# Output products in attention's last steps, and up-weight splits ahead of the last quotient

## The chip, the cores and the metric

One core of one Trainium2 chip runs the kernel. The metric is the device time of one execution in microseconds (us); for a set of runs it is their median. TensorE (PE in the profile) multiplies matrices, ScalarE (ACT) and VectorE (DVE) work on tiles element by element and read TensorE's results from PSUM, GpSimd (POOL) works on tiles in SBUF, and SyncE (SP) issues most of the DMAs.

## The reference

A decoder block on 1024 tokens of width 1024, all in float32:

```python
proj = rmsnorm(h) @ w_in                         # q, k, v, u, gate, forget
att  = forgetting_attention(q, k, v, log_f)      # 8 heads of 64, causal softmax
sg   = chunked_spatial_gating(gelu(u), gelu(gate), ...)
h = h + concat([att, sg]) @ w_out
a, g = split(conv3(rmsnorm(h) @ w_up) + conv_b)  # 2 x 2816 columns
h = h + (silu(g) * a) @ w_down
return rmsnorm(h) * norm_final_g
```

## The kernel before

**Number format.** Every float32 operand of a matmul is split into a high part (a cast) and a low part (source minus high part), and a product is three matmuls: high x high, high x low, low x high. `split_w` makes both parts of a weight tile: the high one on ScalarE (L160), the low one on VectorE (L166). The large projections are done by a Strassen-Winograd scheme on 2 x 2 blocks, so they need sums of blocks of the weights and of the activations (S1 to S4, T1 to T4).

**Attention** runs in 40 steps, five for each of eight heads (`STEPS`). A step n transposes the softmax weights of step n + 1 on TensorE (`turn_p`, L1038); ScalarE (L1039) and VectorE (L1040) split the result into a tile `pt` of three buffers. Then it does the value products of step n (`values`, L1054), and in between the logits of the next head, while there is one (`logits_mm`, L984 and L985). The order on TensorE is written by hand: `seq` chains every matmul to the one before. The last head has no logits beside it, so steps 35 to 39 hold transposes and values alone.

**The quotient.** A head's row sums are transposed (`row_tail`, L941), copied (L942), written to DRAM by a DMA that ScalarE issues (L943), and read back spread over 64 partitions by a DMA on SyncE (L944). `pair_half` divides for two heads: multiply by the reciprocals (L953 or L957), cast (L954 or L958), low part (L955 or L959). Three pairs go through GpSimd; the last, `pair_half(3, ...)`, through VectorE and ScalarE, tokens 512 to 1023 first, then 0 to 511. Its result is `attT[3]`.

**Output projection** (`wmm`, L1303 to L1305). For token tile tt (128 tokens) and half hf (512 columns), four head pairs k of three matmuls each add up in one PSUM bank. The order of the token tiles is 0, 4, 1, 5, 2, 3, 6, 7. For the first four tiles the pairs k = 0, 1, 2, eight groups of nine matmuls, come first; they do not need `attT[3]`. Then, tile by tile: the rest of the products, the addition of the residual (`hadd`, L1313, one operand in PSUM), the norm (`norm2`, L1320 to L1323), and one tile later the transposes of the normed tile (`flip`, L1341) with their evacuations. These matmuls are not chained by `seq`; a planner orders them by its costs.

**First up weights.** `upw_a(i)` loads two blocks of weight column i and `split` splits them (i = 0 and 1 ahead of time) into tiles `wha`. `upw_b(i, ..., True)` then makes four sums for each i on GpSimd (L1275, L1276, L1277, L1283), in place over the raw blocks. `wha` lies in a pool that takes the place of attention's pool `early`, after its release.

**Order.** Queues are in order. Where the code doesn't say, a planner places instructions by its own costs; `after(tc, later, earlier)` adds an edge of order without a semaphore, `behind(inst, key)` the same from a table `gates`, and `act.on = dve.on = True` chains all that follows on these engines.

Of the kernel before, what the change touches and what calls it, by code (L numbers as in the profile page):

```python
# [8 lines left out]
F32 = mybir.dt.float32  # L9
# [60 lines left out]
def block_kernel(ctx: ExitStack, tc: tile.TileContext, xT, xtok, wuv, wuh, wv0, wva, wvk, wvl, wqk, cpk, bfv,  # L70
# [5 lines left out]
    sml = ctx.enter_context(tc.tile_pool(name="sml", bufs=4))  # L76
    early = tc.alloc_tile_pool(name="early", bufs=1)
# [13 lines left out]
    BUFS = {"x1": 2, "x2": 2, "t3": 1, "t2": 1, "t01": 1, "V": 4, "H": 4, "wy": 2, "gg": 2,  # L91
# [4 lines left out]
    def sb(tag, shape, dt=F32):  # L96
        return (raws if tag == "raw" else late if tag in LATE else early).tile(shape, dt, tag=tag, bufs=BUFS[tag], name=nm(tag))

# [58 lines left out]
    def split_w(src, hl, hi_eng="act", lo_eng="dve"):  # L157
        h, l = hl
        if hi_eng == "act":
            act.copy(h, src)  # L160
# [5 lines left out]
        return eng.tensor_tensor(out=l, in0=src, in1=f32(h), op=ALU.subtract)  # L166

    gates = {}
# [9 lines left out]
    def xset(tags):  # L178
        return [sb(t, [P, 2, 2, 512], F32R) for t in tags]
# [5 lines left out]
    def xs(n, hl, k):  # L185
        return XS[n][k // 2][:, hl, k % 2, :]

    def x2(n, hl, j):
        return XS[n][j][:, hl, :, :]
# [433 lines left out]
    def emit(t, dst, i, parts, src=None):  # L623
        for o in parts:
            if dst is kd:
                dve.tensor_tensor(out=t[:, 1, o], in0=t[:, 1, o], in1=rb[:, o], op=ALU.mult)
            x = t[:, 1, o] if src is None else src
            act.copy(t[:, 0, o].bitcast(F32R), x)
            floors[dst is kd] = dve.tensor_tensor(out=t[:, 1, o], in0=x, in1=t[:, 0, o], op=ALU.subtract)
            for j in range(2):  # L630
                floors["sp"] = sp.dma_start(out=dst[2 * i + j].rearrange("s d t -> d s t")[:, :, o], in_=t[j * 64:(j + 1) * 64, :, o])

# [80 lines left out]
    floors = {}  # L713
# [16 lines left out]
    xy = sb("x1", [P, 2, 1024])  # L730
    xl = sb("pt", [P, 1024])
    sp.dma_start(out=xl, in_=vx[0])
    after(tc, sp.dma_start(out=xy, in_=vx[1:3].rearrange("a p c -> p a c")), floors["ld"])
    for i, o in ((0, ALU.subtract), (1, ALU.add)):
        after(tc, dve.tensor_tensor(out=xy[:, i], in0=xy[:, i], in1=xl, op=o), newest[0])
    vw["S1"] = pairs(l21)

# [130 lines left out]
    def head_loads(h):  # L868
        ab = sb("x1", [P, 2, 1024], F32R)
        abs_[h] = ab  # L870
        hh = h % 2
        sp.dma_start(out=f32(ab[:, 0, :]), in_=qd[h].rearrange("s d t -> (s d) t"))
        for s in range(2):
            sp.dma_start(out=f32(ab[s * 64:s * 64 + 64, 1, :]), in_=kd[h, 0])
# [10 lines left out]
    va_, vb_, vc_ = xy[:, 0], xy[:, 1], xl  # L885
# [61 lines left out]
    def pair_half(p, o):  # L947
# [8 lines left out]
        else:  # L956
            dve.tensor_tensor(out=f[:, 0, o], in0=f[:, 0, o], in1=f[:, 1, o], op=ALU.mult)  # L957
# [5 lines left out]
    psa = tc.alloc_tile_pool(name="psb", bufs=4, space=bass.MemoryType.PSUM, reuse_waits="tile")  # L963

    def place():
        return psa.tile([P, 1024], F32, tag="L", bufs=2, name=nm("pl"))
# [9 lines left out]
    def logits_mm(h, j, ps):  # L976
        A, B, A2, B2 = abs_[h][:, 0, :], abs_[h][:, 1, :], a2s[:, h % 2, :], b2s[:, h % 2, :]
# [135 lines left out]

    STEPS = [[(h, g) for g in GROUPS[n:n + 2]] for h in range(8) for n in range(0, 9, 2)]
# [35 lines left out]
    for n, step in enumerate(STEPS):  # L1150
# [33 lines left out]
        out_copy = None  # L1184
        for c, (g, pt, js) in enumerate(zip(step, now, NEXT[s])):
# [30 lines left out]
    for o in (slice(512, 1024), slice(0, 512)):  # L1216
        pair_half(3, o)


    after(tc, act.activation(pad[:, 0:1], eps, AF.Sqrt), last_copy)  # L1220


    ss2 = cst.tile([P, 8], F32, name="ss2")

    early.release()
    psa.release()
    psa = tc.alloc_tile_pool(name="psc", bufs=4, space=bass.MemoryType.PSUM, reuse_waits="tile")
    upl = tc.alloc_tile_pool(name="upl", bufs=1, reuse_waits="tile")
    xtp = tc.alloc_tile_pool(name="xtp", bufs=1, reuse_waits="tile")

    g2b = xtp.tile([P, 1024], F32, name="g2b")
    sp.dma_start(out=g2b, in_=g2r.to_broadcast((P, 1024)))
    XB = {}

    def xb_tile(pool_, n):
        XB[n] = pool_.tile([P, 2, 4, 512], F32R, tag="x" + n, bufs=1, name="x" + n)

    for n in ("B11", "B21", "T2", "T3"):
        xb_tile(upl, n)

    def ut_(pool_, tag, shape, dt, bufs):
        return pool_.tile(shape, dt, tag=tag, bufs=bufs, name=nm(tag))

    xt = {n: xtp.tile([P, 4, 512], F32, tag="xt" + n, name="xt" + n) for n in ("B11", "B21", "B22")}
# [4 lines left out]
    def upw_a(i):  # L1249
# [15 lines left out]
        return out, split  # L1265

# [32 lines left out]
    def wmm(tt, hf, ps, ks_):  # L1299
        ts_ = slice(tt * P, (tt + 1) * P)  # L1300
        for k in ks_:
            w = wo[k][hf]
            pe.matmul(ps, attT[k][:, 0, ts_], w[:, 0, :], start=(k == 0), stop=False)  # L1303
            pe.matmul(ps, attT[k][:, 0, ts_], w[:, 1, :], start=False, stop=False)
            pe.matmul(ps, attT[k][:, 1, ts_], w[:, 0, :], start=False, stop=(k == 3))  # L1305

# [26 lines left out]
    def flip(tt):  # L1333
# [3 lines left out]
        for kh in range(2):  # L1337
            ps = sbank()
            for j in range(4):
                k = 4 * kh + j  # L1340
                pe.transpose(ps[:, j * P:(j + 1) * P], xn[tt][:, k * P:(k + 1) * P], ident)  # L1341
# [58 lines left out]
    def psq(tag):  # L1400
        return psa.tile([P, 512], F32, tag="b" if tag in "ab" else "s", bufs=4, name=nm("q" + tag))
# [217 lines left out]
    banks = [psa.tile([P, 512], F32, tag="b" if j < 4 else "s", bufs=4, name="k%d" % j) for j in range(8)]  # L1619

    RING = {"xr": (upl, "sg", 4), "xh": (upl, "wha", 4), "wh": (upr, "whb", 6)}
# [168 lines left out]
    raws.release()  # L1790
    psa.release()
# [53 lines left out]
```

## Time and profile before

| what | value |
| --- | --- |
| median of 3 runs | 1046.32 us (1046.3 to 1047.15) |
| profiled execution | 1046.16 us, span 1044.4 us |
| mean granted TensorE clock | 0.998 |
| last value products end, first output product starts | about 357.5 us |
| last quotient's parts | 362.4 to 365.0 us |
| first residual addition of the output projection | 374.75 us |
| first products of the up projection | 407.06 us |

The page gives busy times and the chain that ended last; the timeline gives each instruction's start, duration, lines and tiles (`out<-in`), and in brackets how long its engine had idled and what ended that. Start-to-start distances on TensorE tell more than its busy time, since matmuls overlap in the record.

### The profile page before, as it was taken

Reading aid. Unit: us, or ns where it says so; the run is one execution under the profiler, and the core shown is the slowest. Engines: PE = TensorE matmul, PEld = TensorE weight load, DVE = VectorE, ACT = ScalarE, POOL = GpSimd, SP = SyncE. Lnnn points to the kernel's source line nnn. Section 1 sums busy time; section 2 is a strip of 40 time slices with the busy share of each in tenths; the row PEclk is TensorE's granted clock in tenths of the full one; section 3 lists DMA queues with packets and bytes.
Section 4 is the critical chain, followed back from the end, with each engine's and each line's share of the span. In section 5 each row is a group of like instructions: output and inputs, shape, how many; then the busy total and the mean of one; then the engine's idle time right before and its main releaser. Section 6 shows DMA issues by size and latency. Waiting matters only on the chain.

```text
span 1044.4 us, 14270 instructions
## 1 busy us (share of the span) xinstructions
PE 1036.8 (99%) x4998; PEld 870.0 (83%) x4998; DVE 893.3 (86%) x1302; ACT 562.8 (54%) x1003; POOL 222.6 (21%) x167
## 2 busy tenths in 40 slices
PE   9999999999999999999999999999999999999997
PEld 7988888988888888788888888888888888888886
DVE  6899887988888779998999998898997866997774
ACT  6777632457776747644444444443544544454654
POOL 0000232500322540353334323323331000000000
PEclk9999999999999999999999999999999999999999
DMA  9622558885745533231354431332422998333432
GB/s 331 235 85 95 153 156 250 232 259 170 203 135 167 201 134 130 81 120 62 121 168 146 142 121 67 127 111 73 129 81 83 325 337 292 112 92 101 144 118 101
DMA packets 67452, 161.66 MB, mean 155 GB/s; under 512 B 8095, under 2 KB 9239, under 8 KB 67381
## 3 DMA queue, kind: packets, MB, share of 16 engines
q1 hardware_dynamic: 67108, 160.72, 47.9%
q8 instruction: 39, 0.64, 0.3%
q14 instruction: 33, 0.26, 0.1%
q10 hardware_dynamic: 272, 0.04, 0.0%
HBM read 115.68 MB, written 45.05 MB: 154 GB/s over the span
## 4 chain that ended last, share of the span: by engine, by line
PE 98%; DVE 1%; ACT 0%; issue 0%; ACTq 0%; DVEq 0%
PE k L1656 20%; PE qc L1396 12%; PE qa L1396 11%; PE qd L1396 11%; PE qb L1396 5%; PE pb L270 5%; PE ps L270 5%; PE pb L1054 3%; PE pb L1038 3%; PE qc L509 2%; PE qd L509 2%; PE qa L509 2%; PE pl L984 2%; PE ps L853 2%; PE pl L985 2%; PE pf L1078 1%
## 5 line engine op out<-in xcount | busy, mean ns | idle before, releaser
L1656 PE MATMUL k<-whb,wha 128*128 128x512 f32 (+1 forms) x936 | 209.9, 387 | 0.0
L1656 PEld LDWEIGHTS k<-whb,wha 128*128 128x128 f32 x936 | 174.1, 188 | 35.8 <-DVE wha L166 0.2
L1396 PE MATMUL qc<-xT,whb 128*128 128x512 f32 x540 | 129.8, 389 | 0.1
L1396 PE MATMUL qa<-xB,wha 128*128 128x512 f32 x528 | 127.5, 390 | 0.0
L1396 PEld LDWEIGHTS qc<-xT,whb 128*128 128x128 f32 x540 | 101.3, 188 | 21.5 <-ACT whb L160 0.5
L1396 PEld LDWEIGHTS qa<-xB,wha 128*128 128x128 f32 x528 | 98.8, 188 | 20.9 <-DVE wha L166 0.4
L160 ACT CAST wha<-sg 128x512 fp32r<-128x512 f32 x77 | 47.8, 622 | 96.6 <-PE k L1656 84.9
L160 ACT CAST whb<-sg 128x512 fp32r<-128x512 f32 x82 | 50.5, 618 | 87.9 <-PE qc L1396 67.6
L166 DVE TENSOR_TENSOR wha<-sg,wha 128x512 fp32r<-128x512 f32 x77 | 52.8, 688 | 39.0 <-ACT wha L160 38.9
L1396 PE MATMUL qd<-xB,whb 128*128 128x512 f32 x264 | 63.7, 389 | 0.0
L1396 PE MATMUL qd<-xT,whb 128*128 128x512 f32 x264 | 63.7, 390 | 0.0
L1396 PE MATMUL qb<-xT,whb 128*128 128x512 f32 x252 | 61.0, 390 | 0.0
L166 DVE TENSOR_TENSOR whb<-sg,whb 128x512 fp32r<-128x512 f32 x82 | 57.0, 697 | 4.4 <-ACT whb L160 4.3
L1280 POOL TENSOR_TENSOR sg<-raw 128x512 f32<-128x512 f32 x20 | 31.0, 1550 | 139.4 <-DVE whb L166 76.2
L1039 ACT CAST pt<-pb 128x512 fp32r<-128x512 f32 x72 | 40.1, 583 | 36.0 <-PE pb L1038 23.7
L1396 PEld LDWEIGHTS qd<-xT,whb 128*128 128x128 f32 x264 | 49.5, 188 | 10.5 <-DVE u L1503 0.3
L1396 PEld LDWEIGHTS qd<-xB,whb 128*128 128x128 f32 x264 | 49.6, 188 | 10.3
L1396 PEld LDWEIGHTS qb<-xT,whb 128*128 128x128 f32 x252 | 47.2, 188 | 10.0 <-DVE whb L166 0.3
L1040 DVE TENSOR_TENSOR pt<-pb,pt 128x512 fp32r<-128x512 f32 x72 | 47.3, 686 | 9.6 <-ACT pt L1039 8.9
L1054 PE MATMUL pb<-pt,V 128*128 128x512 f32 (+3 forms) x192 | 49.4, 362 | 0.4 <-DVE pt L1040 0.3
L1283 POOL TENSOR_TENSOR sg<-sg,raw 128x512 f32<-128x512 f32 x20 | 33.3, 1664 | 63.5 <-DVE whb L166 63.5
L1281 POOL TENSOR_TENSOR sg<-sg,raw 128x512 f32<-128x512 f32 x20 | 35.1, 1756 | 47.2 <-issue 44.6
(431 smaller groups left out, 2247.6 us busy)
## 6 DMA issues: line engine op xcount, KB each, us to landing
raw<-wup SPq DMA_DIRECT2D x44, 512.0 KB
sg<-hx SPq DMA_DIRECT2D x77, 256.0 KB
hx<-hs SPq DMA_DIRECT2D x44, 256.0 KB
hx<-ca SPq DMA_DIRECT2D x35, 256.0 KB
xT<-wdn SPq DMA_DIRECT2D x28, 256.0 KB
x<-kd SPq DMA_DIRECT2D x24, 256.0 KB
A<-xtok SPq DMA_DIRECT2D x8, 512.0 KB
raw<-wqk SPq DMA_DIRECT2D x8, 512.0 KB
```

The lines of the kernel that those rows point to most:

```text
L160: act.copy(h, src)
L166: return eng.tensor_tensor(out=l, in0=src, in1=f32(h), op=ALU.subtract)
L270: pe.matmul(banks[m], xs(n, xi, k)[:, ms], w[:, wi, :], start=(first and k == 0 and c == 0 and (own or m % 2 == 0)), stop=(k == 3 and c == ...
L509: pe.matmul(ps, w[:, wi, ks], xs(n, xi, k), start=(first and c == 0), stop=(c == 11), skip_group_check=True)
L1038: seq(pe.transpose(ptr[:, o:o + P], places[g[0], j // 2][j % 2][:, k * P:(k + 1) * P], ident))
L1039: casts.append(act.copy(pt[:, 0, :], ptr))
L1040: los.append(dve.tensor_tensor(out=pt[:, 1, :], in0=ptr, in1=f32(pt[:, 0, :]), op=ALU.subtract))
L1054: seq(pe.matmul(po[half][:, o:o + w], lhs, pt[:, s, c:c + w], start=(new and s == 0), stop=(s == 1 and (half, k) in ((1, 6), (0, 3))), ski ...
L1281: pool.tensor_tensor(out=s[1], in0=s[0], in1=a11, op=ALU.add)
L1283: pool.tensor_tensor(out=s[3], in0=s[1], in1=a12, op=ALU.add)
L1396: pe.matmul(ps, w[:, wi, ks], xb[:, xi, k, :], start=(first and n == 0), stop=(n == 11), skip_group_check=True)
L1656: pe.matmul((banks[bk + m] if ps is None else ps)[:, o], xh[:, xi, ms], wh[:, wi, o], start=((first and p_ == 0 or new) and n == 0), stop= ...
```

## The change

- `wmm` moves ahead of the loop over the steps and is chained by `seq`. Token tile 0, half 0, takes its k = 0, 1, 2 in steps 36, 37 and 39, after the transposes and before the values of the step. Its bank comes from a PSUM pool that replaces the one of the logits after their last use.
- After attention only four more groups of nine are done ahead of k = 3: (4, 0), (0, 1), (4, 1) and (1, 0).
- The first up weights (i = 0, 1) are split right behind the last values: their casts come after the last evacuation of values, and the first multiply of the last quotient comes after the last of the four subtractions. The load of the square root's table comes after the last cast. For this the tiles of `wha` move into the pool of the logits' operands (tag `x1`, four buffers of half the size), which stays allocated.
- The flips have written places between half tiles, chained by `seq`, except the last.
- The partial sums of the values are loaded by two DMAs instead of one, ahead of the last six stores of queries and keys; their two additions come behind the last splits and the last query subtraction.

```diff
     def split_w(src, hl, hi_eng="act", lo_eng="dve"):
         if hi_eng == "act":
-            act.copy(h, src)
+            cast[:] = [act.copy(h, src)]
...
-    xy = sb("x1", [P, 2, 1024])
+    xy = [sb("x1", [P, 1024]) for _ in range(2)]
     xl = sb("pt", [P, 1024])
     sp.dma_start(out=xl, in_=vx[0])
-    after(tc, sp.dma_start(out=xy, in_=vx[1:3].rearrange("a p c -> p a c")), floors["ld"])
-    for i, o in ((0, ALU.subtract), (1, ALU.add)):
-        after(tc, dve.tensor_tensor(out=xy[:, i], in0=xy[:, i], in1=xl, op=o), newest[0])
+    for i in range(2):
+        ld = sp.dma_start(out=xy[i], in_=vx[1 + i])
+        after(tc, ld, floors["ld"])
+        for st in stores[-6:]:
+            after(tc, st, ld)
+    adds = [dve.tensor_tensor(out=xy[i], in0=xy[i], in1=xl, op=o) for i, o in ((0, ALU.subtract), (1, ALU.add))]
     vw["S1"] = pairs(l21)
+    for x in adds:
+        after(tc, x, newest[0])
+        after(tc, x, floors[False])
...
         else:
-            dve.tensor_tensor(out=f[:, 0, o], in0=f[:, 0, o], in1=f[:, 1, o], op=ALU.mult)
+            m = dve.tensor_tensor(out=f[:, 0, o], in0=f[:, 0, o], in1=f[:, 1, o], op=ALU.mult)
+            if gates:
+                after(tc, m, gates.pop("own"))
             act.copy(t[:, 0, o], f[:, 0, o])
...
+    def wmm(tt, hf, ps, ks_):
+        ts_ = slice(tt * P, (tt + 1) * P)
+        for k in ks_:
+            w = wo[k][hf]
+            for n, (a, b) in enumerate(((0, 0), (0, 1), (1, 0))):
+                seq(pe.matmul(ps, attT[k][:, a, ts_], w[:, b, :], start=(k == 0 and n == 0), stop=(k == 3 and n == 2)))
+
+    banks8 = {}
+    EARLY = {36: (0,), 37: (1,), 39: (2,)}
...
+        if n == 35:
+            psl.release()
+            psl = tc.alloc_tile_pool(name="psc", bufs=4, space=bass.MemoryType.PSUM, reuse_waits="tile")
+            banks8[0, 0] = lbank()
+        if n in EARLY:
+            wmm(0, 0, banks8[0, 0], EARLY[n])
         for c, (g, pt, js) in enumerate(zip(step, now, NEXT[s])):
...
             for n in names:
-                t = ut_(upl, "wha", [P, 2, 512], F32R, 4)
+                t = ut_(base, "x1", [P, 2, 512], F32R, 4)
                 split_of[n] = split_w(wr[:, ("A11", "A12").index(n), :], (t[:, 0], t[:, 1]))
-                behind(split_of[n], "sums" if i < AHEAD else "hg")
+                if i < AHEAD:
+                    after(tc, cast[0], last_copy)
+                else:
+                    behind(split_of[n], "hg")
...
+    WA = [upw_a(i) for i in range(AHEAD)]
+    W = [a[1](("A11", "A12")) for a in WA]
+    gates["own"] = split_of["A12"]
+    for o in (slice(512, 1024), slice(0, 512)):
+        pair_half(3, o)
+
+
+    after(tc, act.activation(pad[:, 0:1], eps, AF.Sqrt), cast[0])
...
     def flip(tt):
-            ps = sbank()
+            ps = bank()
             for j in range(4):
                 k = 4 * kh + j
-                pe.transpose(ps[:, j * P:(j + 1) * P], xn[tt][:, k * P:(k + 1) * P], ident)
+                t = pe.transpose(ps[:, j * P:(j + 1) * P], xn[tt][:, k * P:(k + 1) * P], ident)
+                if tt < 7:
+                    seq(t)
...
-    WA = [upw_a(i) for i in range(AHEAD)]
-    W = [WA[0][1](("A11", "A12"))]
-    first = (0, 4, 1, 5)
-    banks8 = {(tt, hf): (bank() if hf == 0 else sbank()) for tt in first for hf in range(2)}
-    for hf in range(2):
-        for tt in first:
-            wmm(tt, hf, banks8[tt, hf], (0, 1, 2))
-    W.append(WA[1][1](("A11", "A12")))
+    early_ = ((0, 0), (4, 0), (0, 1), (4, 1), (1, 0))
+    for tt, hf in early_[1:]:
+        banks8[tt, hf] = bank() if tt == 1 else lbank()
+        wmm(tt, hf, banks8[tt, hf], (0, 1, 2))
     WB = [upw_b(0, W[0], True), upw_b(1, W[1], True)]
-    prev = None
+    FLIP = {(1, 1): 0, (5, 0): 4, (2, 0): 1, (3, 0): 5, (6, 0): 2, (7, 0): 3, (7, 1): 6}
     for tt in (0, 4, 1, 5, 2, 3, 6, 7):
         hload(tt)
         for hf in range(2):
-            if tt in first:
-                wmm(tt, hf, banks8[tt, hf], (3,))
-                hadd(tt, hf, banks8[tt, hf])
-            else:
-                ps = bank()
-                wmm(tt, hf, ps, range(4))
-                hadd(tt, hf, ps)
-        norm2(tt)
-        if prev is not None:
-            flip(prev)
-        prev = tt
+            ps = banks8[tt, hf] if (tt, hf) in early_ else bank() if tt == 1 else lbank()
+            wmm(tt, hf, ps, (3,) if (tt, hf) in early_ else range(4))
+            hadd(tt, hf, ps)
+            if hf:
+                norm2(tt)
+            if (tt, hf) in FLIP:
+                flip(FLIP[tt, hf])
```

`lbank()` takes one of four banks of the pool that replaces the logits' places, `bank()` one of the four others.

More of the change, by code (lines that the diff above doesn't have):

```diff
@@ L96, in sb @@
     def sb(tag, shape, dt=F32):
-        return (raws if tag == "raw" else late if tag in LATE else early).tile(shape, dt, tag=tag, bufs=BUFS[tag], name=nm(tag))
+        return (base if tag == "x1" else raws if tag == "raw" else late if tag in LATE else early).tile(shape, dt, tag=tag, bufs=BUFS[tag], name=nm(tag))
     def bank():
@@ L178, in xset @@
     def xset(tags):
[L179 removed]
+        r = []
+        for t in tags:
+            if t == "x1":
+                r.append([sb(t, [P, 2, 512], F32R) for _ in range(2)])
+            else:
+                b = sb(t, [P, 2, 2, 512], F32R)
+                r.append([b[:, 0], b[:, 1]])
+        return r
     RAW = {n: [sb(t, [P, 2, 512]) for t in tags] for n, tags in (
@@ L1618, in block_kernel @@
     ssa = dn.tile([P, 1], F32, name="ssa")
-    banks = [psa.tile([P, 512], F32, tag="b" if j < 4 else "s", bufs=4, name="k%d" % j) for j in range(8)]
-    RING = {"xr": (upl, "sg", 4), "xh": (upl, "wha", 4), "wh": (upr, "whb", 6)}
+    banks = [lbank() if j < 4 else bank() for j in range(8)]
+    RING = {"xr": (upl, "sg", 4), "xh": (base, "x1", 4), "wh": (upr, "whb", 6)}
     def dt_(tag, shape, dt):
```

67 lines of the change are left out of this document (31 added, 36 removed).

## Prediction

> **What bounds the kernel now.** I read the page from the top (busy shares, then the chain that ended last), then what TensorE waited for over the whole span.
>
> ```profile
> span 1044.4 us, 14270 instructions
> PE 1036.8 (99%) x4998; PEld 870.0 (83%) x4998; DVE 893.3 (86%) x1302; ACT 562.8 (54%) x1003; POOL 222.6 (21%) x167
> PE 98%; DVE 1%; ACT 0%; issue 0%; ACTq 0%; DVEq 0%
> PE ps L126 <- DVE pad L137: 1.3, 1, 1.3
> ```
>
> TensorE is the bound, and no instruction of it is removed. A change can only pay by closing small waits and can only cost by opening new ones. "Busy" hides small waits, because a matmul's modelled end overlaps the next; they show as start-to-start steps that are too long. The yardsticks, from the chain, are twelve 512-column matmuls in 2.72 us (0.227 each) and eight transposes in 0.87 us (0.109 each). Here are attention's last steps, first as TensorE's timeline, then as the chain:
>
> ```profile
> 425.34 2.72 PE qd L1396 x12
> 352.87 0.87 PE pb L1038 x8
> ...
> 351.71 1.16 PE L1054 MATMUL pb<-pt,V 128*128 128x512 f32 x4
> 354.68 0.27 PE L941 MATMUL pb<-ident,rs 128*8 128x128 f32 x1
> 357.45 0.45 PE L1303 MATMUL pb<-whl,A 128*128 128x512 f32 x1
> ...
> 354.25 0.60 ACT pt L1039
> 354.87 0.70 DVE pt L1040
> 355.64 0.60 ACT pt L1039
> 356.25 0.70 DVE pt L1040
> ```
>
> From the values of step 36 (351.71) to the first output product (357.45) pass 5.74 us. The work in them is 8 matmuls of 512 columns, 4 of 384, 4 of 256, 4 of 128 and 13 transposes: at 0.227 us in proportion to columns, and 0.109, that is 1.82 + 0.68 + 0.45 + 0.23 + 1.42 = 4.60 us. So 1.1 us is waiting, on the ScalarE cast and VectorE subtraction of the transposed weights, as the chain says.
>
> **The change part by part.**
>
> *Three groups in steps 36, 37 and 39.* Nine products of 0.227 us, 2.04 us in all, leave the stretch after attention and enter these steps. Filled perfectly they would hide 1.1 us; unfilled, 0. I take 0.95: almost all the waiting is late in the stretch, behind the insertions, but the pt ring has three buffers, so a later cast waits for the values just pushed back. Attention then ends at 357.45 + 2.04 - 0.95 = 358.54. The transposed row sums (354.68) stand behind two of the groups: 1.36 us of inserted work, less about 0.15 of covered waits, make the last quotient's transfers about 1.2 us later.
>
> *The last quotient and the up splits.* Before:
>
> ```profile
> 358.87 0.45 SPq L944 DMA_DIRECT2D H<-rsd  x1
> 357.65 0.58 ACT L1062 COPY H<-pb 64x512 f32<-64x512 f32 x1 [0.82 <-PE pb L1054]
> 358.25 1.28 ACT L1220 ACT_TABLE_LOAD   x1
> 358.26 0.68 DVE L1063 TENSOR_TENSOR H<-pb,H 64x512 f32<-64x512 f32 x1 [0.60 <-ACT H L1062]
> 362.36 1.29 DVE L957 TENSOR_TENSOR H<-H 128x512 f32<-128x512 f32 x2 [3.41 <-DMA H<-rsd]
> 363.08 1.22 ACT L958 CAST G<-H 128x512 fp32r<-128x512 f32 x2 [3.33 <-DVE H L957]
> 363.74 1.29 DVE L959 TENSOR_TENSOR G<-H,G 128x512 fp32r<-128x512 f32 x2
> 374.32 0.39 PE L1305 MATMUL pb<-G,G 128*128 128x512 f32 x1
> ```
>
> The quotient is ready at 363.74 + 1.29 = 365.03, and TensorE first reads its low part at 374.32, after 72 products that need only heads 0 to 5. The change leaves 36 between attention's end and that group. TensorE would be there at 358.54 + 36 x 0.227 + 2 x 0.227 = 367.17. Meanwhile the four splits (four casts, four subtractions) come into VectorE's 3.41 us of idling, and the first quotient multiply is ordered behind the last of them. The gap looks as if it holds them: four subtractions at 0.6 us. But what follows the first of them matters:
>
> ```profile
> 364.95 0.68 DVE L166 TENSOR_TENSOR wha<-raw,wha 128x512 fp32r<-128x512 f32 x1
> 366.15 1.78 DVE L166 TENSOR_TENSOR wha<-raw,wha 128x512 fp32r<-128x512 f32 x1
> 367.85 1.77 DVE L166 TENSOR_TENSOR wha<-raw,wha 128x512 fp32r<-128x512 f32 x1
> ...
> 365.71 1.67 POOL L1275 TENSOR_TENSOR raw<-raw,raw 128x512 f32<-128x512 f32 x1 [12.72 <-DMA pt<-hpd]
> 369.04 1.74 POOL L1277 TENSOR_TENSOR raw<-raw 128x512 f32<-128x512 f32 x1
> 370.74 1.29 POOL L1283 TENSOR_TENSOR raw<-sg,raw 128x512 f32<-128x512 f32 x1
> 374.75 0.69 DVE L1313 TENSOR_TENSOR pt<-pb,pt 128x512 f32<-128x512 f32 x1 [5.12 <-PE pb L1305]
> ```
>
> GpSimd's eight sums of up weights overwrite the raw weights in place, so the first starts 0.08 us after the first subtraction ends (365.63). From there the two engines take turns. A subtraction with both inputs in SBUF takes 1.78 us instead of 0.68, and each GpSimd sum 1.67 to 1.74 instead of 1.29 alone. The two ends 367.93 and 369.62 set the period: 1.69 us. The addition that reads PSUM keeps its 0.69 us. Before, only two subtractions that nobody waited for met the sums. In the new order GpSimd starts ahead of the quotient, so two subtractions, both multiplies and both quotient subtractions (two SBUF inputs each) meet them, and eight sums outlast six such turns.
>
> The page "SBUF — State Buffer" of the Trainium skill (section "Who interferes with whom") states the same as a rule: VectorE with two SBUF inputs and a GpSimd read exclude each other, and the later one blocks for the whole instruction. Taking turns at the lone durations, 0.68 + 1.29 = 1.97 us, it would put the sum 5 x 0.28 = 1.4 us higher than the measured turns do.
>
> The sum by measured rows: last copy 358.54 + 0.20 = 358.74; its addition 0.61 later, 359.35; first subtraction from 359.96 to 360.64; third ends 2.30 after the first (365.63 to 367.93), 362.94; fourth 364.63; the multiplies 366.32 and 368.01; the subtractions 369.70 and 371.39. The row sums land at 362.3 + 1.2 = 363.5, ahead of the first multiply, and the casts (0.61) lie beside VectorE's turns. The table load, now behind the casts, ends near 363. TensorE reads the low part at 371.45 instead of 367.17: it stands 4.3 us, some 2 before the first product of the group (its cast ends 0.61 after the second multiply) and the rest before the third.
>
> Against before: at 374.32 TensorE had 74 of these products behind it, at 371.45 it has 47. The missing 27 x 0.227 = 6.13 us bring it level at 377.58, 3.26 us late. That already contains the 0.95 of the first part.
>
> *Norms and flips, in written order.* Work is the same. VectorE's additions begin at about 371.9 (0.43 behind that product, as before) instead of 374.75, while TensorE is 3.3 us later, so VectorE has some 6 us more lead. What can be had here:
>
> ```profile
> 380.38 0.88 PE ps L1341 x8
> 383.55 0.61 PE ps L1341 x4
> 385.79 1.06 PE ps L1341 x8
> ...
> 428.96 0.60 PE qd L1396 x2
> 429.56 0.83 PE qb L1396 x3
> 441.59 0.51 ACT whb L160
> ...
> 416.00:424.00 8.00, 8.00 (x37) 6.62 (x36) 8.00 (x10) 7.34 (x10) 0.00 (x0) 1.00 0.00 0
> ```
>
> Two flips are long by 0.17 and 0.19 us, against 0.44 for four and 0.87 for eight transposes: 0.35 goes. Around 428 to 442 stand 0.15 + 0.15 (two at 0.60, three at 0.83, against 0.227 each) and at most the 0.51 of the cast at 441.59. VectorE is full from 416 on (8.00 of 8.00 in the window), but this follows the last flip, which keeps its place behind TensorE's products, so I take 0, with 0.8 as the bound. The first flip now follows the products of (1, 1), at 377.1, some 3.9 us after token tile 0's second addition ends. Before, from that end (374.75 + 2 x 0.68 = 376.1) to the flip at 380.38 it took 4.3 with other tiles' additions in between, so a wait of 0 to 0.4 can open; VectorE is less crowded, and I take 0.
>
> *Edits at nothing.* The x1 tiles and the split tiles change pools with as many buffers. The value partial sums:
>
> ```profile
> 176.79 0.90 SPq L733 DMA_DIRECT2D x<-vx  x1
> 182.44 4.37 SPq L631 DMA_DIRECT2D kd<-G  x4
> 185.34 0.68 DVE L629 TENSOR_TENSOR G<-G 128x512 f32<-128x512 f32 x1
> 185.94 2.35 DVE L735 TENSOR_TENSOR x<-x,pt 128x1024 f32<-128x1024 f32 x2
> ```
>
> One load becomes two, about 0.9 us more on SyncE's queue; the six stores now ordered behind them issue from 182.44, 4.7 us later anyway. The two additions already run behind the last query subtraction, which becomes their order. If that cover went, the 2.35 us would delay the values' evacuation.
>
> *Sum.* 3.26 - 0.35 = +2.9 us. The profiled execution took 1046.16 us (1.76 around its span) and gives 1049.06; the median, 0.16 above it, gives 1049.2.
>
> **The rivals.**
>
> *GpSimd is out of the way* (its tiles still held by attention's, or its queue ordered otherwise). Then the fourth subtraction ends at 362.5, the quotient at 363.5 + 0.6 + 0.61 + 0.6 + 0.69 = 366.0, before 367.17. What remains is -0.95 - 0.35 = -1.3 us: 1045.0. For it speaks that the trace cannot show which old tile the sums' first output covers; against it, that before nothing but the first subtraction held them. Held for half the window, +0.8: 1047.1.
>
> *VectorE's lead pays* (the other side, faster). Without the collision all small waits go: 1.1 + 0.35 + 0.8 = 2.25 us, and 1044.1 remains. It decides only if the quotient's low part stands by 367.2 and the 0.8 us at 428 to 442 was backlog. VectorE's 8.00 of 8.00 speaks for it, the last flip's place against.
>
> *The fill fills nothing.* The pt ring moves with the inserted products, and 0.95 is lost. This adds 0.95 to each case: 1050.1 with the collision, 1046.0 without.
>
> *A slow clock after the stall.* The clock row shows 1.00 in every window, and the longest wait of the trace is 1.3 us; 4.3 us in two parts is outside what it shows. At the start there is such a phase:
>
> ```profile
> 1.29 3.59 PE ps L126 x8
> ```
>
> The eight warming matmuls and the five after them step by about 0.43 us, 0.2 more each; paying that once is 13 x 0.2 = 2.6 us: 1051.8. The page "TensorE: Matmul & The Clock Gate" of the Trainium skill (Part 1) puts the drop after an idle window of about 3.4 us; each of the two halves is shorter, and no row here tests it.
>
> **How the numbers follow.** Collision as summed 0.53, GpSimd out of the way 0.25, half-way 0.08, VectorE's lead 0.08, slow clock 0.06. A bound of 0.2% is 2.1 us, about what a measurement of this kernel can tell from no change: faster is below 1044.2, slower above 1048.4. Slower: 0.47 of the collision (its own range, by 0.95 of fill and 0.2 us per turn, is 1048.1 to 1050.2; the lowest part, 0.06, falls inside) and 0.06: 0.53. Same: 0.25 + 0.08 + 0.06 = 0.39. Faster: 0.08. The range runs from 1044.4, under the case without collision, to 1050.6; outside lie the fastest case, the slow clock and some tails, under 0.2.
>
> **What would show it.** Right: subtractions of the first up weights from about 360, the later ones near 1.7 us with GpSimd busy beside them; quotient multiplies (128x512, H) also near 1.7 us; TensorE idle about 2 us twice, released by the quotient's cast and then its subtraction; first hidden-state addition near 371.9. Wrong: multiplies at 0.69 us and the first addition near 367.6, or GpSimd's first sum behind the quotient. The fill is right if the first product of token tile 4 starts near 358.5.

## Result: 0.6% slower, and the profile after

The changed kernel takes 1052.83 us (median of 6 runs, 1052.21 to 1053.37) against 1046.46 us before; the ratio is 1.0060 (95% interval 1.0047 to 1.0073). Its profiled execution took 1052.44 us. The forecast was 1049.2, with a range up to 1050.6: the direction was right, but the loss is 6.4 us where 2.9 were forecast, more than twice as much.

The head of the page and TensorE's waits over the whole span (line that waited, line that released it, total us, times, longest us):

```profile
span 1050.7 us, 14270 instructions
PE 1038.0 (99%) x4998; PEld 870.4 (83%) x4998; DVE 896.6 (85%) x1302; ACT 564.6 (54%) x1003; POOL 223.4 (21%) x167
PE pk L1140 <- ACT G L975: 2.0, 1, 2.0
PE pk L1140 <- DVE G L976: 1.9, 1, 1.9
PE pb L838 <- DVE G L55: 1.0, 3, 0.6
```

The busy share of TensorE is 99% in both kernels and shows nothing. The waits do: two at the output products (L1140) for the last quotient, as forecast, and three at L838, the transposes of the gated values ("gate transposes" below), 143 us ahead of the first step that the prediction gives a price (208.6 against 351.7 us).

Around the quotient, VectorE's and GpSimd's timeline:

```profile
361.92 4.68 DVE L167 TENSOR_TENSOR x<-raw,x 128x512 fp32r<-128x512 f32 x4
366.53 3.46 DVE L972 TENSOR_TENSOR H<-H 128x512 f32<-128x512 f32 x2
369.91 3.42 DVE L976 TENSOR_TENSOR G<-H,G 128x512 fp32r<-128x512 f32 x2
374.10 0.69 DVE L1346 TENSOR_TENSOR pt<-pk,pt 128x512 f32<-128x512 f32 x1 [0.78 <-PE pk L1140]
362.69 1.67 POOL L1316 TENSOR_TENSOR raw<-raw,raw 128x512 f32<-128x512 f32 x1 [8.07 <-DVE x L167]
364.44 1.61 POOL L1318 TENSOR_TENSOR raw<-raw 128x512 f32<-128x512 f32 x1
```

Before, two multiplies took 1.29 us and two quotient subtractions 1.29 us; now 3.46 and 3.42. GpSimd's first sum starts 0.08 us behind the first split subtraction (361.92 + 0.69) and from there the engines take turns, as forecast. TensorE's timeline and granted clock at the same place (a row of windows: length, then busy us of PE, PEld, DVE, ACT, POOL with counts, then the granted clock, DMA share, GB/s):

```profile
360.38 0.91 PE L1140 MATMUL pk<-whl,A 128*128 128x512 f32 x3
...
367.95 0.84 PE L1140 MATMUL pb<-G,G 128*128 128x512 f32 x3
370.78 0.70 PE L1140 MATMUL pk<-G,G 128*128 128x512 f32 x2 [1.99 <-ACT G L975]
373.38 4.14 PE L1140 MATMUL pk<-G,G 128*128 128x512 f32 x10 [1.89 <-DVE G L976]
...
372.00:373.00 1.00, 0.00 (x0) 0.00 (x0) 1.00 (x1) 0.00 (x0) 1.00 (x2) 1.00 0.00 0
373.00:374.00 1.00, 0.62 (x2) 0.53 (x3) 0.32 (x1) 0.00 (x0) 1.00 (x1) 0.77 0.00 0
374.00:375.00 1.00, 1.00 (x4) 0.81 (x3) 0.69 (x1) 0.00 (x0) 1.00 (x2) 0.50 0.00 0
375.00:376.00 1.00, 1.00 (x4) 0.71 (x4) 0.62 (x1) 0.00 (x0) 0.70 (x1) 0.50 0.00 0
376.00:377.00 1.00, 1.00 (x4) 0.81 (x3) 0.41 (x2) 0.89 (x1) 0.00 (x0) 0.53 0.13 49
377.00:378.00 1.00, 1.00 (x6) 0.82 (x5) 0.80 (x2) 0.55 (x3) 0.00 (x0) 1.00 1.00 401
```

Ten products of 512 columns take 4.14 us where twelve took 2.72. Seven of them step by 0.427 us instead of 0.227, the first by 0.48. The clock column sums up to 0.23 + 0.50 + 0.50 + 0.47 = 1.70 us lost, that is 3.4 us at half clock.

Where the time went is read by counting TensorE's matmuls (4998 in both records): the n-th of the changed kernel starts so much later than the n-th before. The columns are the growth of that offset in five stretches (in us; the start of the span varies by itself from run to run). Three experiments, e6, e11 and e12, add matmuls and are left out of this count.

| kernel | up to n = 1000 (197 us) | to 1100: gate transposes | 1900 to 2000: steps with the fill | 2000 to 2018: quotient's products | to 2600: flips | sum at 4900 |
| --- | --- | --- | --- | --- | --- | --- |
| the change | 0.14 | 1.49 | -0.75 | 6.02 | -0.71 | 6.14 |
| sides swapped (e1) | 0.85 | 0.02 | -0.81 | 6.06 | -0.75 | 5.33 |
| half of the sums held (e2) | 0.33 | 1.50 | -0.79 | 2.49 | 0.02 | 3.62 |
| sides and half of the sums (e4) | 0.14 | 0.00 | -0.77 | 2.49 | 0.03 | 1.81 |
| splits behind (e3) | 0.18 | 1.49 | -0.81 | 4.49 | -0.67 | 4.74 |
| all sums held (e5) | 0.23 | 1.52 | -0.77 | 0.00 | -0.63 | 0.28 |
| no fill (e7) | 0.11 | 1.50 | -0.01 | 4.03 | -0.65 | 4.94 |
| sides and sums (e8) | -0.37 | 0.01 | -0.79 | 0.00 | -0.58 | -1.76 |
| the same, no fill (e9) | 0.52 | 0.00 | -0.03 | 0.00 | -0.53 | -0.01 |
| the same, splits behind (e10) | 0.75 | 0.02 | -0.75 | 0.00 | -0.71 | -0.70 |

### The profile page after: what moved, and what is told of

It reads as the page before. It is cut to its first block, busy times and chain, and to the rows that moved or that the text cites. A ratio compares the mean times of both kernels' runs of the same rounds, so it can differ in the third digit from the quotient of the medians.

```text
span 1050.7 us, 14270 instructions
## 1 busy us (share of the span) xinstructions
PE 1038.0 (99%) x4998; PEld 870.4 (83%) x4998; DVE 896.6 (85%) x1302; ACT 564.6 (54%) x1003; POOL 223.4 (21%) x167
## 4 chain that ended last, share of the span: by engine, by line
PE 96%; DVE 2%; DMA 1%; ACT 1%; issue 0%; SPq 0%; DVEq 0%; ACTq 0%
PE pb L1423 22%; PE pk L1423 17%; PE pb L1683 11%; PE pk L1683 9%; PE ps L278 5%; PE pb L278 5%; PE pb L1075 3%; PE pk L1140 3%; PE pb L1059 3%; PE qc L517 2%; PE qd L517 2%; PE qa L517 2%; PE pl L1005 2%; PE ps L868 2%; PE pl L1006 2%; PE pf L1099 1%
## 5 line engine op out<-in xcount | busy, mean ns | idle before, releaser
L1423 PE MATMUL pb<-xT,whb 128*128 128x512 f32 x804 | 189.7, 389 | 0.2 <-ACT whb L161 0.2
L1423 PEld LDWEIGHTS pb<-xT,whb 128*128 128x128 f32 x804 | 150.8, 188 | 31.9 <-ACT whb L161 0.5
L1423 PE MATMUL pk<-xB,x 128*128 128x512 f32 x528 | 127.2, 390 | 0.0
L1683 PE MATMUL pb<-whb,x 128*128 128x512 f32 (+1 forms) x528 | 119.2, 387 | 0.0
L1423 PEld LDWEIGHTS pk<-xB,x 128*128 128x128 f32 x528 | 98.8, 188 | 20.8 <-DVE x L167 0.4
L1683 PEld LDWEIGHTS pb<-whb,x 128*128 128x128 f32 x528 | 98.3, 188 | 20.3 <-DVE x L167 0.2
L1683 PE MATMUL pk<-whb,x 128*128 128x512 f32 (+1 forms) x408 | 91.8, 386 | 0.0
L1683 PEld LDWEIGHTS pk<-whb,x 128*128 128x128 f32 x408 | 75.9, 188 | 15.5
L1423 PE MATMUL pb<-xB,whb 128*128 128x512 f32 x264 | 63.7, 389 | 0.0
L1423 PE MATMUL pk<-xT,whb 128*128 128x512 f32 x252 | 61.0, 390 | 0.0
```

Source lines behind the costliest of these rows:

```text
L1423: pe.matmul(ps, w[:, wi, ks], xb[:, xi, k, :], start=(first and n == 0), stop=(n == 11), skip_group_check=True)
L1683: pe.matmul((banks[bk + m] if ps is None else ps)[:, o], xh[:, xi, ms], wh[:, wi, o], start=((first and p_ == 0 or new) and n == 0), stop= ...
```

## The experiments

All are edits of the changed kernel, each timed beside the kernel before on the same chip. They ran on several chips, on which the kernel before took 1046.30 to 1046.51 us in the median; where two experiments differ by 1 us or less, their ratios to the kernel before and the table say more than their medians. The theory: 1.5 us is a matter of PSUM banks at L838; 4.2 us is the collision of VectorE and GpSimd; 1.65 us is the clock, halved by TensorE's idling in it.

### e1: the two PSUM pools change sides

The change splits attention's PSUM pool in two, one for the four-bank ring `b` and one for the two wide places of the logits. In one pool the places, taken first, had banks 0 to 3 and the ring 4 to 7. In two pools the ring, made first, lies on 0 to 3, where the first batch of gate transposes has just been. The bank numbers are read from the order in which the code makes the pools; no trace names a bank.

```diff
-    psa = tc.alloc_tile_pool(name="psb", bufs=4, space=bass.MemoryType.PSUM, reuse_waits="tile")
+    psa = tc.alloc_tile_pool(name="psb", bufs=4, space=bass.MemoryType.PSUM, reuse_waits="tile", side="right")
```

> The changed kernel with one edit: the PSUM pools of attention swap sides, so that the four-bank ring b lies on banks 4 to 7 again, as before the change, and the two wide places on 0 to 3. Every engine's instructions and their order stay. In the changed kernel TensorE falls 1.5 us behind between 208.1 and 211, in the second batch of gate transposes (L838), each waiting for a subtraction of the first batch's low part. Theory 'bank placement': the four transposes now take the banks that the first batch used last; with the sides swapped the waits go, the gate transposes run 0.87 us per eight, and the time falls by 1.5 us, 1052.8 to 1051.3. The stall before the last quotient's products (2.0 and 1.9 us) stays, since everything behind shifts alike. Rival 'loads and stores': the 1.5 us come from the two value-sum loads, the six ordered stores and the additions ahead of this place; then nothing changes, 1052.8, and TensorE still stands at L838.

1051.61 us (1051.36 to 1052.38), ratio 1.0049 (1.0036 to 1.0062): 1.2 us less. Every queue holds the same instructions in the same order. TensorE's timeline of the gate transposes, first before (L823 there), then of the change, then of e1:

```profile
206.39 1.91 PE L823 MATMUL ps<-ident,A 128*128 128x128 f32 x16
208.14 1.91 PE L823 MATMUL pb<-ident,A 128*128 128x128 f32 x16
```

```profile
206.74 1.69 PE L838 MATMUL ps<-ident,A 128*128 128x128 f32 x14
208.62 0.63 PE L838 MATMUL pb<-ident,A 128*128 128x128 f32 x4 [0.18 <-DVE G L55]
209.47 0.63 PE L838 MATMUL pb<-ident,A 128*128 128x128 f32 x4 [0.22 <-DVE G L55]
210.67 1.06 PE L838 MATMUL pb<-ident,A 128*128 128x128 f32 x8 [0.57 <-DVE G L55]
```

```profile
207.24 1.91 PE L838 MATMUL ps<-ident,A 128*128 128x128 f32 x16
208.98 1.91 PE L838 MATMUL pb<-ident,A 128*128 128x128 f32 x16
```

In the change each wait ends with a VectorE subtraction that reads the first batch (`G L55`). In e1 the second batch runs without a break, as before, and the 1.49 us of the table become 0.02. The median moved by 0.3 us less, and the profiled execution started 0.7 us later by n = 1000, ahead of the edit. The loads and stores of the value sums cost nothing that these profiles can show: the offset at n = 1000, behind them, is within the spread of the start in all the runs.

### e2 and e5: GpSimd's sums behind the quotient

e2 puts two GpSimd copies that read the quotient's low part ahead of the sums in the text; e5 also orders the sums behind the second copy.

```diff
+    held_ = [pool.tensor_copy(pad[:, 0:1], f32(attT[3][:, 1, o:o + 1])) for o in (512, 0)]
...
-            pool.tensor_tensor(out=a11, in0=a21, in1=a11, op=ALU.add)
-            pool.tensor_tensor(out=s[1], in0=a11, in1=a22, op=ALU.add)
-            pool.tensor_tensor(out=a21, in0=a21, in1=a22, op=ALU.add)
+            for o, a, b in ((a11, a21, a11), (s[1], a11, a22), (a21, a21, a22)):
+                after(tc, pool.tensor_tensor(out=o, in0=a, in1=b, op=ALU.add), held_[1])
```

> The changed kernel with one edit: two one-column GpSimd copies that read the last quotient's low part stand ahead of GpSimd's eight sums of up weights, so that the sums start behind the quotient. The four up splits stay ahead of it. Theory 'taking turns': subtractions and multiplies of VectorE fall from 1.75 to 0.69 us, the low part is ready near 367.0 instead of 373.3, TensorE comes to it at 368.6 and does not stand; the 4.2 us of stall go and with them the seven products at half pace (1.65 us): 1052.8 - 5.85 = 1047.0. Rival 'the splits themselves': four splits ahead of the quotient are what makes it late; then multiplies take 0.69 us but TensorE still stands 1 us or more: 1048 or above. Rival 'the half pace is not of the stall' (a property of this place, such as the first products on a fresh bank): the stall goes and seven products still step by 0.427 us: 1048.6.

e2 took 1050.23 us (1049.92 to 1050.71), ratio 1.0037 (1.0023 to 1.0050), 3.2 above its expectation. The planner placed four of the sums ahead of the copies, so half of the collision stayed: the groups show the multiplies still at 1767 ns and only the quotient's subtractions at 694.

```profile
L972 DVE TENSOR_TENSOR H<-H 128x512 f32<-128x512 f32 x2 | 3.5, 1767 | 0.0
L976 DVE TENSOR_TENSOR G<-H,G 128x512 fp32r<-128x512 f32 x2 | 1.4, 694 | 0.1
370.96 3.22 PE L1140 MATMUL pk<-G,G 128*128 128x512 f32 x12 [1.99 <-ACT G L975]
378.12 1.07 PE L1374 MATMUL pb<-ident,xn 128*128 128x128 f32 x8 [0.53 <-DVE ss L1355]
```

TensorE stands once instead of twice, no slow products follow, and the first flip now waits for its norm, which takes the flips' gain back. This says nothing yet on the rival that blames the splits; e5 does.

> The changed kernel with all eight GpSimd sums of up weights behind the last quotient's low part (where the four sums that need one half of the weights alone had slipped ahead, half of the collision was left). Splits ahead of the quotient, pools, early products and flips as changed. Theory 'taking turns': no VectorE instruction between 362 and 368 takes over 0.95 us, the four splits end near 364.5, the multiplies start when the row sums have landed (365.5 in the run with half the collision), the low part is ready near 368.1, TensorE comes to it at 369.1 and does not stand; 4.2 + 1.65 us go, 0.7 us come back as a wait of the first flip for its norm, which the half run showed: 1052.8 - 5.15 = 1047.7. Rival 'the splits themselves': TensorE still stands over 0.5 us at the first product: 1048.5 or above. Rival 'late row sums': they land after 366.5 and a stall of 0.5 us or more stays.

1047.03 us (1046.51 to 1048.41, 11 runs), ratio 1.0006 (0.9998 to 1.0015): 5.8 us less than the change by this one edit. The timeline of VectorE, with one of GpSimd's sums, then TensorE's:

```profile
362.01 2.50 DVE L167 TENSOR_TENSOR x<-raw,x 128x512 fp32r<-128x512 f32 x4
364.42 1.28 DVE L972 TENSOR_TENSOR H<-H 128x512 f32<-128x512 f32 x2
365.79 1.30 DVE L976 TENSOR_TENSOR G<-H,G 128x512 fp32r<-128x512 f32 x2
369.60 2.05 DVE L1347 TENSOR_TENSOR pt<-pk,pt 128x512 f32<-128x512 f32 x3 [2.51 <-PE pk L1140]
369.85 1.29 POOL L1319 TENSOR_TENSOR sg<-raw,raw 128x512 f32<-128x512 f32 x1
...
368.04 0.84 PE L1140 MATMUL pb<-G,G 128*128 128x512 f32 x3
368.72 2.88 PE L1140 MATMUL pk<-G,G 128*128 128x512 f32 x12
```

The same eight instructions take 5.1 us from first start to last end (362.01 to 367.09) instead of 11.4 (361.92 to 373.33). The quotient is ready at 367.1, TensorE comes at 368.7 and does not stand. Splits ahead of the quotient are harmless alone. The row sums have landed by 364.42 here; in the change the multiplies follow the splits at 366.53 without a wait, so the row sums are not what holds the quotient there. The 0.7 us that the expectation added for the flip did not come.

### e3 and e10: the up splits behind the quotient again

```diff
     for o in (slice(512, 1024), slice(0, 512)):
         pair_half(3, o)
-    after(tc, act.activation(pad[:, 0:1], eps, AF.Sqrt), cast[0])
+    after(tc, act.activation(pad[:, 0:1], eps, AF.Sqrt), last_copy)
+    W = [a[1](("A11", "A12")) for a in WA]
```

> The changed kernel with the four up splits put back behind the last quotient (the table load ahead of the quotient's casts again); early products, pools and flips stay as changed. GpSimd's sums follow the splits in place, so they come behind the quotient too. Theory 'taking turns': the multiplies start when the row sums land, near 363.5, take 0.69 us, the low part is ready near 366.1, TensorE does not stand: 1052.8 - 5.85 = 1047.0, as with GpSimd held alone. Rival 'the splits themselves': this one gains more than holding GpSimd, by 1 us or more. Rival 'late row sums': the multiplies start later than 365.5 because the transfers of the row sums are late, and a stall of 1 us or more stays.

1049.68 us (1048.90 to 1051.27), ratio 1.0033 (1.0020 to 1.0046): a miss, by 2.7 us. The planner let one split go ahead while VectorE waited for the row sums, and that was enough to release GpSimd's sums of the first weight column. The first two ran while VectorE waited; the third (366.67, 1.74 us) met the multiplies and the fourth (369.70, 1.59 us) the quotient's subtractions. VectorE's timeline:

```profile
363.28 0.69 DVE L167 TENSOR_TENSOR x<-raw,x 128x512 fp32r<-128x512 f32 x1 [1.34 <-ACT x L161]
366.32 2.64 DVE L972 TENSOR_TENSOR H<-H 128x512 f32<-128x512 f32 x2 [2.35 <-DMA H<-rsd]
368.88 0.68 DVE L167 TENSOR_TENSOR x<-raw,x 128x512 fp32r<-128x512 f32 x1
369.49 2.35 DVE L976 TENSOR_TENSOR G<-H,G 128x512 fp32r<-128x512 f32 x2
```

Two waits stayed (0.93 and 1.43 us), with slow products behind them in the profiled execution. The rival 'late row sums' has its two signs, but the collision has a part in the stall: the multiplies start at 366.32, when the row sums land, 6.0 us after their load was issued (360.27), where before it took 3.5 (358.87 to 362.36), 4.0 in e9 and 5.0 in e10. Why it took longer was not tried.

> Both repairs with the four up splits put back behind the quotient's multiplies, beside the 1045.4 with the splits ahead. Theory: with GpSimd held the place of the splits is worth nothing, since TensorE stands at the quotient in neither: 1045.4, within 0.3. Rival 'the splits ahead pay': behind the quotient they push VectorE's first additions back and open a wait at the first flip: 1046 or above.

With GpSimd held and the sides swapped, 1045.56 us (1044.91 to 1046.60), ratio 0.9992 (0.9983 to 1.0001), against 1045.42 with the splits ahead (e8): the place of the splits is worth nothing that these runs can show.

### e6, e11 and e12: what halves the clock

Added products with operands long ready, into a bank that nobody reads; e6 has eight in both waits, e11 eight in the first alone, e12 nine in the first and one in the second.

```diff
+    def dummy(ps, n):
+        for i in range(n):
+            seq(pe.matmul(ps, attT[0][:, 0, 0:P], wo[0][0][:, 0, :], start=True, stop=True))
...
+            if (tt, hf) == (0, 0):
+                idle = bank()
+                dummy(idle, 8)
+                ts_, w = slice(0, P), wo[3][0]
+                for n, (a, b) in enumerate(((0, 0), (0, 1), (1, 0))):
+                    if n == 2:
+                        dummy(idle, 8)
+                    seq(pe.matmul(ps, attT[3][:, a, ts_], w[:, b, :], start=False, stop=(n == 2)))
+            else:
+                wmm(tt, hf, ps, (3,) if (tt, hf) in early_ else range(4))
```

> The changed kernel with eight added products (512 columns, heads 0 and 1, written to a bank that nobody reads) in each of TensorE's two waits, some 1.8 us of work in 2.15 and 2.06 us. The collision, the splits and the two waits for cast and subtraction stay; only TensorE's idleness goes. Theory 'idleness slows the clock': the products behind step by 0.227 us from the first, the granted clock stays at 1.00, 1.65 us go, of which the first flip's wait may take back 0.7: 1051.2 to 1051.9. Rival 'the half pace belongs to the place' (the operands just written, the banks): seven products still step by 0.427 us and the time stays at 1052.8.

1050.90 us (1050.32 to 1051.80), ratio 1.0044 (1.0032 to 1.0057), 1.9 us less than the change, though TensorE does 16 products more and waits for the same releases. The windows, of e6:

```profile
373.00:374.00 1.00, 0.88 (x5) 0.42 (x4) 0.78 (x1) 0.00 (x0) 1.00 (x2) 1.00 0.00 0
374.00:375.00 1.00, 1.00 (x5) 0.82 (x6) 0.63 (x1) 0.00 (x0) 1.00 (x2) 1.00 0.00 0
375.00:376.00 1.00, 1.00 (x6) 0.81 (x5) 1.00 (x3) 0.21 (x1) 1.00 (x1) 1.00 0.00 0
```

Full clock throughout: the half pace comes of TensorE's idleness, not of the operands or the banks at this place.

> The changed kernel with eight added products in the first of TensorE's two waits only (512 columns, heads 0 and 1, to a bank that nobody reads); the second wait, 2.06 us for the quotient's subtraction, stays idle. Theory 'a share of a stretch': half pace came where TensorE was idle for 2.2 us or more of the 3.4 us before it (in two waits, or in one of 2.1 us after two short ones), and not where it stood once for 2.15 us; with 2.06 us plus the 0.3 us left of the first wait, this is at that edge: the products keep 0.227 us and the time is 1050.9, as with both waits filled, or some of the runs are 1.65 us above the others. Rival 'any wait of 2 us': half pace as before, 1052.5 in every run. Rival 'only idle time without a break counts' is told apart by neither, as no wait here reaches 3.4 us.

1052.12 us (1051.79 to 1053.05), ratio 1.0056 (1.0043 to 1.0068). The first wait kept 0.20 us, the second 1.93, and the slow products came: the theory's 1050.9 failed, and 'any wait of 2 us' came nearer.

> The changed kernel with nine added products in the first of TensorE's two waits (0.1 us of it stay idle) and one in the second, so that it stands once for some 1.85 us, 1.95 us in all. So far the seven slow products came after 2.3 and 2.45 us of idling (one wait of 2.09 us behind 0.2 to 0.36 us) and after more, and did not come in the profile of a single wait of 2.15 us. Theory 'a share of a stretch': 1.95 us is too little, the products step by 0.227 us: 1050.9. Rival 'the place of the wait on the clock's own grid': the single wait of 2.15 us was spared by where it fell; then slow products come here too, in some or all runs: 1052.5 where they do.

1051.07 us (1050.55 to 1053.28), ratio 1.0043 (1.0029 to 1.0057). The profiled execution is the one of 1053.28; the other four lie between 1050.55 and 1051.48. Its wait and its clock, and then the wait and the clock of e2:

```profile
374.22 0.50 PE L1417 MATMUL pk<-G,G 128*128 128x512 f32 x1 [1.69 <-DVE G L976]
...
374.00:375.00 1.00, 0.78 (x3) 0.64 (x4) 0.41 (x2) 0.00 (x0) 1.00 (x1) 0.82 0.00 0
375.00:376.00 1.00, 1.00 (x4) 0.81 (x3) 0.45 (x2) 0.00 (x0) 1.00 (x2) 0.50 0.00 0
```

```profile
370.96 3.22 PE L1140 MATMUL pk<-G,G 128*128 128x512 f32 x12 [1.99 <-ACT G L975]
...
371.00:372.00 1.00, 1.00 (x4) 0.56 (x5) 0.56 (x1) 0.00 (x0) 0.33 (x3) 1.00 0.00 0
372.00:373.00 1.00, 1.00 (x6) 0.82 (x5) 0.84 (x2) 0.00 (x0) 1.00 (x1) 1.00 0.00 0
```

A wait of 1.69 us brought half clock here, and one of 1.99 us did not there. So no length of wait between these decides. The idle share of any 3.4 us does not either: the idlest 3.4 us near the quotient have 2.47 us of idling in e2, which kept its clock, and 2.19 in e12.

What fits every trace is the idle share of one period of the clock's own grid. In every trace the changes of the granted clock lie whole periods of 3.413 us apart. The last change of each trace comes after the last product; these are its windows, first in the change, then in e2:

```profile
1049.00:1050.00 1.00, 0.00 (x0) 0.00 (x0) 0.00 (x0) 0.00 (x0) 0.00 (x0) 0.69 0.20 82
1046.00:1047.00 1.00, 0.00 (x0) 0.00 (x0) 0.00 (x0) 0.00 (x0) 0.00 (x0) 0.80 0.69 283
```

In the change half clock runs from 373.53 to 376.95 us, one period, and again from 1049.37, which is 197 periods later. So the grid of each trace can be laid out, and TensorE's idle time counted in each period, with 0.227 us of work for a product of 512 columns. In the period at whose end the clock fell, TensorE idled 2.81 us (the change), 2.79 (e1), 2.54 (e11), 2.35 (e3), 2.30 (e7) and 2.19 (e12). In e2 the last change is at 1046.60; the grid therefore has a border 198 periods earlier, at 370.76, which cuts the wait, and the period before it has 1.96 us of idling. In e4 the idlest period has 1.85. There the clock did not fall, and no other period at full clock in any trace reaches 1.7. This rests on one profile of each kernel, and the border between falling and not falling lies somewhere between 1.96 and 2.19 us.

### e7 and e9: without the fill

```diff
-    EARLY = {36: (0,), 37: (1,), 39: (2,)}
+    EARLY = {}
...
```

Token tile 0's nine products follow attention again, ahead of the four other groups.

> The changed kernel without the three early groups: all of the first tile's nine products stand behind attention. The fill closed 0.75 us of waits in the trace. Theory 'the chain to the quotient sets the end of the stall': attention and with it the splits and the quotient come 1.29 us earlier (2.04 less 0.75), TensorE comes to the last heads' products 0.75 us later, so the two waits shrink from 4.2 to 2.2 us and become one, the one before the third product; one wait of 2.2 us slowed no clock in the run with half the collision, so the half pace goes too: 1052.8 - 1.3 - 1.65 = 1049.9, faster without the fill. Rival 'the clock slows after any 2 us wait': 1051.5. Rival 'the fill is worth its 0.75 wherever it stands': 1053.6.

1051.26 us (1050.98 to 1052.20), ratio 1.0049 (1.0036 to 1.0063): 1.6 us faster without the fill in the medians, 1.2 in the table (the intervals of the two ratios overlap). The main wait is one of 1.92 us, as the theory said, but the slow products came (the rival's 1051.5):

```profile
369.51 0.70 PE L1140 MATMUL pk<-G,G 128*128 128x512 f32 x2
372.13 4.15 PE L1140 MATMUL pk<-G,G 128*128 128x512 f32 x10 [1.92 <-DVE G L976]
```

With the collision in place the fill costs, since it moves attention's end, and with it the chain that TensorE waits for.

> Both repairs (PSUM sides swapped, all GpSimd sums behind the quotient) without the three early groups, beside the 1045.4 of both repairs with them. Theory 'the fill is worth what it closes once nothing stands behind it': TensorE does not stand at the quotient in either, so leaving the fill out costs the 0.75 us of waits in attention's last steps (a wait of 0.55 us at a 384-column value product returns): 1046.2. Rival 'the fill pays nothing': attention ends 1.3 us earlier without it and VectorE's lead over the flips makes up for it: 1045.4.

1046.57 us (1045.55 to 1047.59), ratio 0.9999 (0.9990 to 1.0007), against 1045.42 with the fill: once nothing stands behind it, the fill is worth 0.8 us in the table and 1.1 in the medians, though the intervals of the two ratios touch.

### e8: both repairs

The edits of e1 and e5 together.

> Both repairs in full: PSUM sides swapped, all eight GpSimd sums behind the quotient's low part. Against the run with the sides swapped and half of the sums held (1048.5), whose TensorE stood 2.15 us for the quotient's cast: that wait goes, the first flip's wait of 0.7 us stays: 1046.4, level with the kernel before (1046.5). Rival 'the splits themselves': a wait of 0.5 to 2 us stays: 1046.9 to 1048.5.

1045.42 us (1044.54 to 1045.90, 11 runs), ratio 0.9990 (0.9981 to 0.9998): faster than both kernels, by 1.0 and 7.4 us, and 1.0 us better than expected, since the first flip does not wait (-0.58 in the table). An earlier form (e4) with e2's half repair took 1048.54 us (1047.70 to 1049.32), ratio 1.0019 (1.0010 to 1.0028); its expectation:

> The changed kernel with both edits: the PSUM sides swapped and GpSimd's sums behind the last quotient. Theory: the gains add, 1052.8 - 1.5 - 5.85 = 1045.5, 1.0 us under the kernel before; what is left of the change is the fill (0.75) and the flips (0.7) less 0.14 at the start. Rival 'given back later': with TensorE earlier, VectorE has less lead over the flips, the 0.7 us there goes again or new waits open: 1046.2 to 1047.

That one missed by 3.0 us, for e2's reason.

## Why the prediction was wrong

- *Three groups in steps 36, 37 and 39*: nearly right. 0.95 was taken; 0.75 to 0.81 is the step in every profile that has the fill. The first product of token tile 4, forecast at 358.54, starts at 360.38, of which 1.64 us were lost upstream.
- *The collision*: right in mechanism and size. GpSimd starts 0.08 us behind the first subtraction, multiplies and subtractions take 1.7 us, TensorE stands from 368.63 (three products from 367.95) to 370.78 and from 371.3 to 373.38, 4.2 us; 4.3 was forecast. e5 shows it by removal.
- *"Edits at nothing"*: the step that failed first. It lists the moved SBUF tiles, loads, stores and additions, and these show no cost: e8 has them all and is 1.0 us below the kernel before. It leaves out the PSUM pools. The same number of banks in the same rings was taken for the same banks; the ring's first four tiles came to lie on the four banks that had been used last, and 1.5 us were lost where no instruction had changed. e1 shows it by moving the ring.
- *A slow clock after the stall*: a rival of 0.06, and it happened. The step leaned on a threshold: the page "TensorE: Matmul & The Clock Gate" of the Trainium skill (Part 1) puts the drop after an idle window of about 3.4 us, and each half of the stall is shorter. Here 2.2 us of idling within one period of the clock's grid were enough (e12), and the stall put 2.8 us into one. The price of 2.6 us (13 products) was too high: 3.4 us at half clock cost 1.7, and the table's 6.02 less 4.2 of waiting gives 1.8.
- *Norms and flips*: -0.35 was taken, -0.71 came: 0.37 up to the 2193rd matmul (405.8 us before) and the rest behind it, 0.16 of it where the small waits stood at 427 to 433 us, so VectorE's lead does pay some of the 0.8 us given as bound. The new wait of the first flip, taken as 0, is 0 in the change.
- *The sum*: 2.9 was -0.95 + 4.2 - 0.35. Measured: 0.14 - 0.75 + 6.02 - 0.71 - 0.05 for the rest, and 1.49, together 6.14. Bank order (1.5) and clock (1.8) are the miss, and neither alone explains it: with the banks mended the time is 1051.61 (e1), with the clock kept up 1050.90 (e6), both above the 1050.6 of the range. The fill's 0.2 less and the flips' 0.36 more nearly cancel.
- The rival *GpSimd is out of the way* (1045.0) describes e8 (1045.42), once the banks are mended too.

## What to carry to other kernels

When a PSUM pool is split, merged or allocated in another order, compare the bank of each tile around the seam, not the count: the first tiles should take the banks that have been free longest. Before filling an engine's idle time, ask which other engine the moved work releases, and hold every instruction of that engine with a real dependency on the work to be protected: a copy placed ahead in the text held half of the sums (e2), and splits placed behind let half of them go once one split slipped forward (e3). Price a stall that leaves TensorE idle for some 2 us within 3.4 with a possible 3.4 us at half clock behind it (1.7 us more here).

## What the runs showed of the hardware

- Half clock lasted the same time whatever came before: in the windows of the change 1.70 us of clock were lost, 3.4 us at half, and 1.70 or 1.71 in e1, e3, e7, e11 and e12. It came after waits of 1.99 and 1.89 us, after 0.93 and 1.43 (e3), after main waits of 1.92 (e7), 1.93 (e11) and 1.69 (e12), and not after one of 1.99 (e2 and e4). What tells these apart is the grid of 3.413 us: at 2.19 us or more of idling in one of its periods the clock fell, at 1.96 or less it did not. In e12 one execution of five is 1.8 us or more above the others; that the grid lay otherwise in those four is not shown. The page of the Trainium skill named above has the window run freely, not tied to the kernel, which fits this: the record of full clock begins 3.97 (e3) to 6.91 us (e7) after the start of the span. That an idle window of full length is needed does not fit.
- VectorE with two SBUF inputs and GpSimd take turns of about 1.7 us (3.46 and 3.42 for two), less than their lone durations in e5 add up to (0.69 + 1.29 = 1.98), which is what whole instructions excluding each other would take (the Trainium skill, "SBUF — State Buffer", "Who interferes with whom"). An addition that reads PSUM is not slowed and slows nothing: in e5 three take 2.05 us beside a GpSimd sum of 1.29.
